# A hybrid decoder trunk on one core: the first modulation summed on two engines and in halves, and the first column block begun on half of the features

## The chip, the cores and the metric

The kernel runs on one core of a Trainium2 chip. A core has TensorE (PE; its weight loads are shown apart as PEld), VectorE (DVE), ScalarE (ACT), GpSimd (POOL), and SyncE (SP), which in this kernel issues every DMA transfer. The metric is the device time of one execution in microseconds (us).

## The reference

One layer over 2048 tokens of 1024 features, batch 1. The part that the change touches is the modulation, the first normalisation and the first projection:

```python
c_act = jax.nn.silu(c)
mod = c_act @ w_ada[l] + b_ada[l]
sh1, sc1, gt1, sh2, sc2, gt2 = [m[:, None, :] for m in jnp.split(mod, 6, axis=-1)]
h = rms_norm(x, g_mix[l]) * (1.0 + sc1) + sh1
p = h @ w_in          # 1024 x 3088, columns shared out among all head groups
```

Behind it come forgetting attention, a chunked mLSTM and a spatial gate over the columns of p, `w_out`, and a ConvFFN with the second modulation. `w_ada` has 1024 rows and 6 x 1024 columns: the first 1024 are the shift `sh1`, the next 1024 the scale `sc1`. All inputs and the output are float32.

## The kernel before

The whole kernel is one stream of instructions for each engine; a scheduler of the framework orders them by priority and dependence, and each engine then runs its own in order. SP keeps eight loads in flight: load number i is issued once load number i - 8 has landed.

**Products.** Each float32 operand of a projection is split into a high part and a rest (`hh` and `hl` for the activations, `whi` and `wlo` for the weights), and `mm3` makes three matmuls of it (lines 54, 55, 56) into one PSUM tile.

**Front.** Four tiles of x (128 tokens x 1024) are loaded and normalised in place (`norm_x`: two squares with a sum on ScalarE, line 498, three small operations, and the product on VectorE, line 503). `first_mod(hf)` (lines 440 to 450) makes shift and scale for features hf * 512 to hf * 512 + 511: for each of the two column ranges, eight tiles `wa` (128 rows of `w_ada` x 512 columns, 256 KB) are loaded; VectorE sums them, weighted by silu(c), into `modacc` (lines 422 and 424); then four matmuls with a column of ones (line 444) sum over the partitions and leave the result as columns. `columns` loads `g_mix` and `b_ada` and transposes them (line 397). VectorE adds the bias (lines 448 to 450) and leaves `sh1` and `a1` (shown as sh and a).

**h tiles.** `make_h(tb, ...)` makes the eight feature tiles k of token block tb (512 tokens): four transposes of x to a PSUM tile (line 542), ScalarE multiplies by `a1` and adds `sh1` (line 546), VectorE makes `hh` (547) and `hl` (548). In token block 0 the PSUM tiles come in turn from `trp` (two buffers) and from `acc` (two buffers and one `acc2`).

**Column blocks.** W_in's columns are taken in 14 blocks, over the first 1024 tokens (half 0) and then over the rest. `w_block` loads a block's weights in two parts `wst` (features 0 to 511 and 512 to 1023); ScalarE makes `whi` (line 569), another engine `wlo` (line 570): GpSimd for the very first block, VectorE for all others. Block 0 of half 0 (272 columns) is `natural` with `use_km`: for each of eight token tiles 8 feature tiles x 3 matmuls of 128 x 272 into one PSUM tile `acc`, an eviction on ScalarE (line 604), a store, and the gates' sum on VectorE (606). Block 1 is `do_qm`. Token block 1's h tiles (x tiles xt4 to xt7) are made between block 0's matmuls. `head_setup` loads a dozen small operands and transposes `wsn`.

**Order of the front before:** `first_mod(0)`, then `w_block(blocks[0][0], G)`, then `first_mod(1)`, then `make_h` of both token blocks with `head_setup` between them, then block 0.

Of the kernel before, what the change touches and what calls it, by code (L numbers as in the profile page):

```python
# [33 lines left out]
def trunk(  # L34
# [403 lines left out]
    modp = mps()  # L438

    def first_mod(hf):  # L440
        for n in (hf, 2 + hf):
            acc = mod_sum(load_ada(n * 512, "hT"))
            for j in range(4):
                T.matmul(modp[:, n * 4 + j : n * 4 + j + 1], acc[:, j * P : (j + 1) * P], ones[:, 0:1], start=True, stop=True)
        if hf == 0:
            columns(colA[:, 0:24], 24, g_mix, b_ada[:, 0:2048])
        sl, o = slice(hf * 4, hf * 4 + 4), hf * 4
        V.tensor_tensor(sh1[:, sl], modp[:, o : o + 4], ba[:, o : o + 4], op=ALU.add)
        V.tensor_tensor(a1[:, sl], modp[:, 8 + o : 12 + o], ba[:, 8 + o : 12 + o], op=ALU.add)
        V.scalar_tensor_tensor(a1[:, sl], a1[:, sl], 1.0, gm[:, o : o + 4], op0=ALU.add, op1=ALU.mult)  # L450
# [86 lines left out]
    def make_h(tb, xin=None):  # L537
        xs = xin if tb == 0 else norm_x(xin or [load_x(tb * 4 + i) for i in range(4)])
        for k in range(KT):
            ps = (tr_ps, acc_ps)[k % 2]() if tb == 0 else tr_ps()  # L540
# [11 lines left out]
    def w_block(parts, eng=V):  # L552

        width = sum(w for _, w in parts)
        tiles = []
        for kp in range(2):
            st = pool.tile([P, 1088], F32, name="wst", tag="wst")
            hi = pool.tile([P, 1088], F32R, name="whi", tag="whi")
            lo = pool.tile([P, 1088], F32R, name="wlo", tag="wlo")
            n = 4 * width  # L560
            v3 = lambda t: t[:, :n].rearrange("p (a b) -> p a b", a=4)
            o = 0
            for col, wd in parts:
                dma(
                    v3(st)[:, :, o : o + wd],
                    w_in[kp * 512 : kp * 512 + 512, col : col + wd].rearrange("(a p) n -> p a n", p=P),
                )
                o += wd
            A.copy(hi[:, :n], st[:, :n])
            eng.tensor_tensor(lo[:, :n], st[:, :n], hi[:, :n].bitcast(F32), op=ALU.subtract)  # L570
            tiles += [(v3(hi)[:, a, :], v3(lo)[:, a, :]) for a in range(4)]
        return tiles, width
# [370 lines left out]
    for n, (half, i) in enumerate(steps):  # L943
        if i == 0:
            make_h(half * 2, x0)
            if half == 0:
                head_setup()
# [658 lines left out]
```

## Time and profile before

| | us |
|---|---|
| median of 3 runs | 2734.72 |
| lowest and highest of the runs | 2733.98, 2736.56 |
| the profiled execution | 2737.65 |
| its span | 2735.9 |

The profiled execution is one of its own, 2.93 us above the median of the runs; 1.75 us of it lie around the span. Its mean granted TensorE clock is 0.978. Busy time is told by engine; times in the timeline count from the start of the span, and a number in brackets there is the time for which the engine stood idle ahead of that row, with what ended it. The front that the change touches is the first 76 us; the rest of the projection, the attention and the ConvFFN follow.

### The profile page before, as it was taken

To read this page: it belongs to the slowest core of one execution; us is meant where nothing else is said; L and a number is where in the kernel's file an instruction comes from. 1 tells how busy PE (TensorE), PEld (TensorE's weight loads), DVE (VectorE), ACT (ScalarE), POOL (GpSimd) and SP (SyncE) were. 2 spreads that over 40 slices of the span, in tenths; PEclk is the share of its full clock that TensorE was granted. 3 is DMA by queue.
4 is the path that set the end of the run, shared out by engine and by line. 5 is a ranking of instruction groups with operands and counts; after the bars stand their busy time and mean duration, and the time that the engine had idled before them with its cause. 6 is when DMAs were issued, how large, how long until landed. Compare 5 with 4: busy or idle time off the path is not lost.

```text
span 2735.9 us, 40287 instructions
## 1 busy us (share of the span) xinstructions
PE 2600.8 (95%) x14345; PEld 2231.9 (82%) x14345; DVE 2009.3 (73%) x3499; ACT 1298.6 (47%) x2448; POOL 459.3 (17%) x592
## 2 busy tenths in 40 slices
PE   5988888989899999999998999999999999999999
PEld 5988888989897788777786888888888888888787
DVE  7356466245446888886668988887988887899797
ACT  4243225233226888884445544444544444444443
POOL 2032221032225566662000000000000000000000
PEclk9988999999999999999999999999999999999999
DMA  7534365424346335625663222228222224849533
GB/s 249 169 102 134 103 183 169 123 53 140 89 139 171 108 108 143 165 56 183 229 242 85 93 90 80 85 82 293 87 78 92 77 85 157 299 137 310 175 108 116
DMA packets 313085, 382.09 MB, mean 140 GB/s; under 512 B 31004, under 2 KB 214264, under 8 KB 310836
## 3 DMA queue, kind: packets, MB, share of 16 engines
q1 hardware_dynamic: 312884, 379.52, 44.2%
q8 instruction: 113, 1.85, 0.3%
q14 instruction: 88, 0.72, 0.1%
HBM read 278.67 MB, written 100.77 MB: 139 GB/s over the span
## 4 chain that ended last, share of the span: by engine, by line
PE 58%; DVE 7%; DMA 2%; ACT 2%; issue 2%; POOL 1%; DVEq 0%; ACTq 0%; SPq 0%; POOLq 0%
PE ub L56 10%; PE ub L55 10%; PE ub L54 10%; PE db L55 4%; PE db L56 4%; PE db L54 4%; PE sp L210 3%; PE tp L263 3%; PE op L249 2%; PE op L250 2%; PE wps L55 2%; PE wps L56 2%; PE wps L54 2%; DVE wspl L1350 2%; DMA wd<-in_w_down_dram 1%
## 5 line engine op out<-in xcount | busy, mean ns | idle before, releaser
L54 PE MATMUL acc<-whi,hh 128*128 128x256 f32 (+1 forms) x1408 | 424.0, 302 | 23.9 <-DVE qn L700 10.8
L56 PE MATMUL acc<-whi,hl 128*128 128x256 f32 (+1 forms) x1408 | 412.0, 294 | 0.5 <-DVE hl L548 0.5
L55 PE MATMUL acc<-wlo,hh 128*128 128x256 f32 (+1 forms) x1408 | 412.2, 293 | 0.0
L54 PEld LDWEIGHTS acc<-whi,hh 128*128 128x128 f32 x1408 | 282.7, 201 | 30.8 <-ACT ev L640 7.5
L55 PEld LDWEIGHTS acc<-wlo,hh 128*128 128x128 f32 x1408 | 283.3, 201 | 0.4 <-issue 0.2
L56 PEld LDWEIGHTS acc<-whi,hl 128*128 128x128 f32 x1408 | 281.9, 201 | 1.3 <-DVE hl L548 0.9
L54 PE MATMUL ub<-T,wsph 128*128 128x512 f32 x704 | 274.2, 390 | 5.8 <-ACT wsph L1218 5.8
L56 PE MATMUL ub<-T,wspl 128*128 128x512 f32 x704 | 273.7, 389 | 0.6 <-DVE wspl L1219 0.6
L55 PE MATMUL ub<-T,wsph 128*128 128x512 f32 x704 | 273.9, 389 | 0.0
L55 PE MATMUL db<-wspl,wsph 128*128 128x512 f32 x616 | 240.4, 390 | 2.7 <-DVE wspl L1350 2.7
L56 PE MATMUL db<-wsph,wspl 128*128 128x512 f32 x616 | 239.6, 389 | 0.0
L54 PE MATMUL db<-wsph 128*128 128x512 f32 x616 | 238.2, 389 | 0.3 <-ACT wsph L1349 0.3
L1218 ACT CAST wsph<-S 128x512 fp32r<-128x512 f32 x176 | 109.7, 623 | 229.6 <-PE ub L55 164.1
L267 DVE TENSOR_TENSOR plo<-tp,phi 128x512 fp32r<-128x512 f32 (+1 forms) x320 | 186.8, 607 | 34.6 <-ACT phi L266 32.6
L54 PE MATMUL ub<-B,wsph 128*128 128x512 f32 x528 | 207.1, 392 | 2.8 <-ACT wsph L1218 2.8
L56 PE MATMUL ub<-B,wspl 128*128 128x512 f32 x528 | 207.0, 392 | 0.7 <-DVE wspl L1219 0.7
L55 PE MATMUL ub<-B,wsph 128*128 128x512 f32 x528 | 206.8, 392 | 0.0
L227 ACT ACTIVATE L<-L,nm 128x1024 f32<-128x1024 f32 (+2 forms) x192 | 172.5, 902 | 33.5 <-DVE nm L216 32.1
L263 PE MATMUL tp<-ident,L 128*128 128x128 f32 x1088 | 180.4, 278 | 3.8 <-POOL L L232 1.2
L266 ACT CAST phi<-tp 128x512 fp32r<-128x512 f32 (+1 forms) x320 | 160.4, 521 | 45.2 <-PE tp L263 43.8
L210 PE MATMUL sp<-kk,q 128*128 128x512 f32 (+3 forms) x640 | 169.3, 376 | 2.4 <-DVE nm L216 1.5
L232 POOL TENSOR_SCALAR L<-L,rs 128x1024 f32<-128x1024 f32 (+2 forms) x192 | 167.2, 881 | 11.2
(334 smaller groups left out, 5891.1 us busy)
## 6 DMA issues: line engine op xcount, KB each, us to landing
w<-in_w_up_dram SPq DMA_DIRECT2D x88, 512.0 KB
wd<-in_w_down_dram SPq DMA_DIRECT2D x176, 256.0 KB
wa<-in_w_ada_dram SPq DMA_DIRECT2D x96, 256.0 KB
wst<-in_w_in_dram SPq DMA_DIRECT2D x48, 512.0 KB
act_d<-yc SPq DMA_DIRECT2D x44, 512.0 KB
act<-act_d SPq DMA_DIRECT2D x44, 512.0 KB
q<-q_d SPq DMA_DIRECT2D x128, 128.0 KB
hc_d<-hl SPq DMA_DIRECT2D x28, 512.0 KB
```

Of the source, the lines that this page charges most:

```text
L54: T.matmul(ps, lh, rh, start=start, stop=False, skip_group_check=resume)
L55: T.matmul(ps, lh, rl, start=False, stop=False, skip_group_check=resume)
L56: T.matmul(ps, ll, rh, start=False, stop=stop, skip_group_check=resume)
L210: T.matmul(sp[:, b : b + bw], q2[n][:, qs], kk[:, s0 + b : s0 + b + bw], start=n == 0, stop=n == 1 and not last)
L227: A.activation(L[c], L[c], AF.Exp, bias=nm[:, n - 1 : n], scale=-1.0, accum_out=rs[:, c : c + 1])
L232: G.tensor_scalar(t, t, rs[:, 0:1], 1.0, op0=ALU.mult, op1=ALU.mult)
L249: T.matmul(op[:, c0:], vv[:, j, :], hi[:, c0:], start=(j == 0), stop=False)
L250: T.matmul(op[:, c0:], vv[:, j, :], lo[:, c0:], start=False, stop=(j == ns - 1))
L263: T.transpose(tp[:, i * P : (i + 1) * P], rows[i][j // 8][:, (j % 8) * P : (j % 8 + 1) * P], ident)
L266: A.copy(hi[:, c0:], tp[:, c0:])
L267: V.tensor_tensor(lo[:, c0:], tp[:, c0:], hi[:, c0:].bitcast(F32), op=ALU.subtract)
L1218: A.copy(hi, src)
```

## The change

`first_mod` loads the shift's and the scale's tiles in turn and keeps the sixteen of a half together. VectorE sums the shift's as before. The scale is summed on TensorE: a 128 x 128 piece of `wa` is the stationary operand, the column of silu(c) that belongs to its rows the moving one, and the eight row tiles accumulate in PSUM (line 451 of the changed kernel), two columns of the result at a time, in a tile `mps` and a tile `mp`; VectorE adds the bias to each (line 454). `columns` of `g_mix` and `b_ada` goes ahead of the tiles. `make_h` takes a range of feature tiles. Token block 0's feature tiles 0 to 3 are made after the first half; the first part of block 0's weights follows, and the matmuls of feature tiles 0 to 3 of three token tiles (36, into all three `acc` buffers); then `first_mod(1)`, the second part of the weights, and feature tiles 4 to 7. `natural` goes on with the three begun PSUM tiles. `wlo` of the first block is made on VectorE. Line numbers of the changed kernel are higher by 10 in `make_h` (542 is 552, 546 is 556), by 8 in the split of the weights (569 is 577, 570 is 578) and by 17 in `use_km` (604 is 621).

```diff
@@ -435,19 +435,29 @@
         V.tensor_scalar(gq8, colA[:, 32:33], 0.125, None, op0=ALU.mult)
 
 
-    modp = mps()
 
     def first_mod(hf):
-        for n in (hf, 2 + hf):
-            acc = mod_sum(load_ada(n * 512, "hT"))
-            for j in range(4):
-                T.matmul(modp[:, n * 4 + j : n * 4 + j + 1], acc[:, j * P : (j + 1) * P], ones[:, 0:1], start=True, stop=True)
         if hf == 0:
             columns(colA[:, 0:24], 24, g_mix, b_ada[:, 0:2048])
-        sl, o = slice(hf * 4, hf * 4 + 4), hf * 4
-        V.tensor_tensor(sh1[:, sl], modp[:, o : o + 4], ba[:, o : o + 4], op=ALU.add)
-        V.tensor_tensor(a1[:, sl], modp[:, 8 + o : 12 + o], ba[:, 8 + o : 12 + o], op=ALU.add)
-        V.scalar_tensor_tensor(a1[:, sl], a1[:, sl], 1.0, gm[:, o : o + 4], op0=ALU.add, op1=ALU.mult)
+        o = hf * 4
+
+        ws = [(next(a_), next(b_)) for a_, b_ in [(load_ada(hf * 512, "hT"), load_ada((2 + hf) * 512, "hT"))] for _ in range(KT)]
+        acc = mod_sum(w for w, _ in ws)
+        for pair in range(2):
+            ps = [mps(), misc_ps()]
+            for k in range(KT):
+                for i in range(2):
+                    c = (2 * pair + i) * P
+                    T.matmul(ps[i][:, 0:1], ws[k][1][:, c : c + P], cs[:, k : k + 1], start=k == 0, stop=k == KT - 1)
+            for i in range(2):
+                c = o + 2 * pair + i
+                V.tensor_tensor(a1[:, c : c + 1], ps[i][:, 0:1], ba[:, 8 + c : 9 + c], op=ALU.add)
+        ps = mps()
+        for j in range(4):
+            T.matmul(ps[:, j : j + 1], acc[:, j * P : (j + 1) * P], ones[:, 0:1], start=True, stop=True)
+        V.tensor_tensor(sh1[:, o : o + 4], ps[:, 0:4], ba[:, o : o + 4], op=ALU.add)
+        sl = slice(o, o + 4)
+        V.scalar_tensor_tensor(a1[:, sl], a1[:, sl], 1.0, gm[:, sl], op0=ALU.add, op1=ALU.mult)
 
     def rest_of_mod(n):
 
@@ -534,10 +544,10 @@
 
     hT = {}
 
-    def make_h(tb, xin=None):
+    def make_h(tb, xin=None, ks=range(KT)):
         xs = xin if tb == 0 else norm_x(xin or [load_x(tb * 4 + i) for i in range(4)])
-        for k in range(KT):
-            ps = (tr_ps, acc_ps)[k % 2]() if tb == 0 else tr_ps()
+        for k in ks:
+            ps = (tr_ps, acc_ps)[k % 2]() if tb == 0 and ks[0] == 0 else tr_ps()
             for i in range(4):
                 T.transpose(ps[:, i * P : (i + 1) * P], xs[i][:, k * P : (k + 1) * P], ident)
             h32 = pool.tile([P, TB], F32, name="h32", tag="t2k")
@@ -549,27 +559,27 @@
             hT[tb, k] = (hh, hl)
 
 
-    def w_block(parts, eng=V):
+    def w_part(parts, kp, eng=V):
 
         width = sum(w for _, w in parts)
-        tiles = []
-        for kp in range(2):
-            st = pool.tile([P, 1088], F32, name="wst", tag="wst")
-            hi = pool.tile([P, 1088], F32R, name="whi", tag="whi")
-            lo = pool.tile([P, 1088], F32R, name="wlo", tag="wlo")
-            n = 4 * width
-            v3 = lambda t: t[:, :n].rearrange("p (a b) -> p a b", a=4)
-            o = 0
-            for col, wd in parts:
-                dma(
-                    v3(st)[:, :, o : o + wd],
-                    w_in[kp * 512 : kp * 512 + 512, col : col + wd].rearrange("(a p) n -> p a n", p=P),
-                )
-                o += wd
-            A.copy(hi[:, :n], st[:, :n])
-            eng.tensor_tensor(lo[:, :n], st[:, :n], hi[:, :n].bitcast(F32), op=ALU.subtract)
-            tiles += [(v3(hi)[:, a, :], v3(lo)[:, a, :]) for a in range(4)]
-        return tiles, width
+        st = pool.tile([P, 1088], F32, name="wst", tag="wst")
+        hi = pool.tile([P, 1088], F32R, name="whi", tag="whi")
+        lo = pool.tile([P, 1088], F32R, name="wlo", tag="wlo")
+        n = 4 * width
+        v3 = lambda t: t[:, :n].rearrange("p (a b) -> p a b", a=4)
+        o = 0
+        for col, wd in parts:
+            dma(
+                v3(st)[:, :, o : o + wd],
+                w_in[kp * 512 : kp * 512 + 512, col : col + wd].rearrange("(a p) n -> p a n", p=P),
+            )
+            o += wd
+        A.copy(hi[:, :n], st[:, :n])
+        eng.tensor_tensor(lo[:, :n], st[:, :n], hi[:, :n].bitcast(F32), op=ALU.subtract)
+        return [(v3(hi)[:, a, :], v3(lo)[:, a, :]) for a in range(4)]
+
+    def w_block(parts):
+        return w_part(parts, 0) + w_part(parts, 1), sum(w for _, w in parts)
 
     pending = []
     background = []
@@ -580,15 +590,22 @@
         if background and (pool.has("att_r") or ticks[0] * 4 % 7 < 4) and next(background[0], True):
             background.pop(0)
 
-    def natural(half, wb, consume):
+    def nat_mm(ps, tt, tiles, width, ks=range(KT)):
+        tb, o = tt // 4, (tt % 4) * P
+        for k in ks:
+            hh, hl = hT[tb, k]
+            mm3(ps[:, :width], hh[:, o : o + P], hl[:, o : o + P], tiles[k][0], tiles[k][1], k == 0, k == KT - 1)
+
+    def natural(half, wb, consume, begun=()):
         tiles, width = wb
         for i in range(8):
             tt = half * 8 + i
-            tb, o = tt // 4, (tt % 4) * P
-            ps = acc_ps()
-            for k in range(KT):
-                hh, hl = hT[tb, k]
-                mm3(ps[:, :width], hh[:, o : o + P], hl[:, o : o + P], tiles[k][0], tiles[k][1], k == 0, k == KT - 1)
+            if i < len(begun):
+                ps = begun[i]
+                nat_mm(ps, tt, tiles, width, range(4, KT))
+            else:
+                ps = acc_ps()
+                nat_mm(ps, tt, tiles, width)
             tick()
             late = consume(tt, ps)
             if late is not None:
@@ -938,13 +955,21 @@
     nb = len(blocks)
     steps = [(h, i) for h in range(2) for i in range(nb)]
     rest = [2, 3, 4, 5, 0, 1, 6, 7]
-    wb = w_block(blocks[0][0], G)
+
+    make_h(0, x0, range(4))
+    wb = w_part(blocks[0][0], 0), 272
+    begun = [acc_ps() for _ in range(3)]
+    for tt in range(3):
+        nat_mm(begun[tt], tt, *wb, range(4))
     first_mod(1)
+    wb = wb[0] + w_part(blocks[0][0], 1), 272
     for n, (half, i) in enumerate(steps):
         if i == 0:
-            make_h(half * 2, x0)
             if half == 0:
+                make_h(0, x0, range(4, KT))
                 head_setup()
+            else:
+                make_h(half * 2, x0)
             make_h(half * 2 + 1)
         elif n == nb - 1:
             x0 = [load_x(8 + t) for t in range(4)]
@@ -965,7 +990,10 @@
         cur = wb
         if n + 1 < len(steps):
             wb = w_block(blocks[steps[n + 1][1]][0])
-        blocks[i][1](half, cur)
+        if n == 0:
+            natural(0, cur, use_km, begun)
+        else:
+            blocks[i][1](half, cur)
         if i == 1:
             log_gates(half)
         if i == 3:
```

Three places, from the instruction lists of the two kernels (a row's number counts the rows of its engine; x8 means eight alike in a row; names are output<-inputs).

TensorE, from the transposes of x2 (k = 0 to 3) to the end of the first half's sums. Before:

```order
14 L542 MATMUL trp<-ident,xt 128x128
15 L542 MATMUL acc<-ident,xt 128x128
16 L542 MATMUL trp<-ident,xt 128x128
17 L542 MATMUL acc<-ident,xt 128x128 x2
18 L444 MATMUL mps<-ones,modacc 128x1 x8
19 L397 MATMUL mp<-ident,rows 128x24
20 L444 MATMUL mps<-ones,modacc 128x1 x4
21 L542 MATMUL trp<-ident,xt 128x128 x4
```

And in the changed kernel (cs is silu(c)):

```order
14 L552 MATMUL acc<-ident,xt 128x128
15 L451 MATMUL mps<-cs,wa 128x1
16 L451 MATMUL mp<-cs,wa 128x1
17 L451 MATMUL mps<-cs,wa 128x1
18 L552 MATMUL trp<-ident,xt 128x128
19 L552 MATMUL acc<-ident,xt 128x128
20 L552 MATMUL trp<-ident,xt 128x128
21 L552 MATMUL acc<-ident,xt 128x128
22 L451 MATMUL mps<-cs,wa 128x1
23 L451 MATMUL mp<-cs,wa 128x1
24 L451 MATMUL mps<-cs,wa 128x1 x2
25 L451 MATMUL mp<-cs,wa 128x1
```

Twenty-one of the first half's 24 matmuls of the first three columns stand behind the four transposes of x3; the rest of them follows in the same pattern.

TensorE, from the end of the first half to the begun matmuls, in the changed kernel:

```order
36 L451 MATMUL mps<-cs,wa 128x1
37 L457 MATMUL mps<-ones,modacc 128x1 x4
38 L451 MATMUL mp<-cs,wa 128x1 x8
39 L552 MATMUL trp<-ident,xt 128x128 x8
40 L54 MATMUL acc<-whi,hh 128x272 x3
41 L55 MATMUL acc<-wlo,hh 128x272
42 L56 MATMUL acc<-whi,hl 128x272
```

Behind the 36 begun matmuls (rows 40 to 73) the second half's sums stand in the same order: 24 of line 451, four of line 457, eight of line 451, and then the transposes of k = 6. The four transposes of k = 4 and of k = 5 are row 39.

ScalarE, from the first h tile. Before:

```order
6 L569 CAST whi<-wst 128x1088 x2
7 L546 ACTIVATE h_384<-trp,sh_90,a_89 128x512
8 L546 ACTIVATE h_395<-acc,sh_90,a_89 128x512
9 L546 ACTIVATE h_406<-trp,sh_90,a_89 128x512
10 L546 ACTIVATE h_417<-acc,sh_90,a_89 128x512
11 L546 ACTIVATE h_428<-trp,sh_90,a_89 128x512
```

And in the changed kernel:

```order
6 L556 ACTIVATE h_335<-trp,sh_90,a_89 128x512
7 L556 ACTIVATE h_346<-acc,sh_90,a_89 128x512
8 L556 ACTIVATE h_357<-trp,sh_90,a_89 128x512
9 L556 ACTIVATE h_368<-acc,sh_90,a_89 128x512
10 L577 CAST whi<-wst 128x1088 x2
11 L556 ACTIVATE h_520<-trp,sh_90,a_89 128x512
```

The two casts of block 0's weights stand behind four h tiles where they stood ahead of them. VectorE's two splits stand there behind the fourth `hh`, and its second half's sums behind the splits.

Further on, the evictions of token tiles 0 and 1 stand on ScalarE ahead of the squares of xt5, where before one eviction stood there; on TensorE nine matmuls of one token tile lie between the last six groups of four transposes of xt4 to xt7, where before the matmuls of two token tiles were interleaved with them. On SP eight small loads of `head_setup` (g_ffn to gmo) stand ahead of the second half's sixteen `wa`, where they stood behind them, and `columns` of `g_mix` and `b_ada` ahead of the first half's.

## The prediction

> **What bounds the kernel now.** I read the page first, then the stretches of the front, then its timeline.
>
> ```profile
> span 2735.9 us, 40287 instructions
> PE 2600.8 (95%) x14345; PEld 2231.9 (82%) x14345; DVE 2009.3 (73%) x3499; ACT 1298.6 (47%) x2448; POOL 459.3 (17%) x592
> ```
>
> TensorE is busy for 95% of the span, so there is time to win where it stands idle. The next view cuts the front into stretches: length, then busy time (and instructions) of PE, PEld, DVE, ACT and POOL, granted clock, DMA share, GB/s.
>
> ```profile
> 0.00:20.00 20.00, 6.65 (x27) 4.99 (x27) 13.09 (x39) 7.86 (x19) 5.20 (x14) 1.00 0.91 332
> 20.00:35.00 15.00, 2.87 (x13) 2.64 (x13) 12.31 (x19) 3.64 (x4) 5.61 (x2) 1.00 0.99 333
> 35.00:40.00 5.00, 4.53 (x20) 4.13 (x20) 4.89 (x9) 1.25 (x2) 0.00 (x0) 1.00 0.19 53
> 43.00:50.00 7.00, 6.96 (x29) 6.01 (x29) 6.29 (x16) 2.78 (x4) 2.31 (x4) 0.51 0.99 364
> 60.00:76.35 16.35, 16.33 (x130) 15.90 (x129) 10.72 (x23) 8.73 (x14) 0.00 (x0) 1.00 0.44 132
> ```
>
> From 20 to 35 us TensorE works 2.87 of 15 us while the DMA engines are 99% busy: the front is a load. From 43 to 50 it is busy at a granted clock of 0.51; from 60 on it is full (16.33 of 16.35). My yardstick is the first matmul of `do_qm`, since behind it the order of instructions stays nearly as it was and TensorE is the bound:
>
> ```profile
> 76.35 0.40 PE L54 MATMUL acc<-hh,whi 128*128 128x512 f32 x1
> ```
>
> The timeline of the front (start, length, engine, line; in brackets the idle time before and who ended it):
>
> ```profile
> 14.80 0.75 DVE L503 TENSOR_SCALAR xt<-xt,st 128x1024 f32<-128x1024 f32 x1 [0.44 <-POOL st L132]
> 15.61 0.47 PE L542 MATMUL trp<-ident,xt 128*128 128x128 f32 x1 [1.39 <-DVE xt L503]
> 18.10 8.23 DVE L424 SCALAR_TENSOR_TENSOR modacc<-wa,cs,modacc 128x512 f32<-128x512 f32 x8
> 19.24 10.85 SPq L414 DMA_DIRECT2D wa<-in_w_ada_dram  x16
> 23.05 5.61 POOL L570 TENSOR_TENSOR wlo<-wst,whi 128x1088 fp32r<-128x1088 f32 x2 [8.29 <-ACT whi L569]
> 23.48 2.85 DVE L424 SCALAR_TENSOR_TENSOR modacc<-wa,cs,modacc 128x512 f32<-128x512 f32 x1
> 23.80 1.10 ACT L569 CAST whi<-wst 128x1088 fp32r<-128x1088 f32 x1 [0.82 <-DMA wst<-in_w_in_dram]
> 29.26 0.78 ACT L546 ACTIVATE h<-trp,sh,a 128x512 f32<-128x512 f32 x1 [4.37 <-DVE a L450]
> 29.60 5.47 DVE L424 SCALAR_TENSOR_TENSOR modacc<-wa,cs,modacc 128x512 f32<-128x512 f32 x7
> 41.61 0.74 DVE L424 SCALAR_TENSOR_TENSOR modacc<-wa,cs,modacc 128x512 f32<-128x512 f32 x1
> 44.72 0.78 ACT L546 ACTIVATE h<-trp,sh,a 128x512 f32<-128x512 f32 x1 [4.42 <-DVE a L450]
> ```
>
> The first h waits until 29.26 for VectorE's sums, although SP, which keeps eight loads in flight, was issuing the second half's at 19.24. At 10.85/16 = 0.68 us a load the first half's last tile landed at about 19.9; VectorE ended 6.4 us later (18.10 + 8.23 = 26.33). The fifth feature tile waits until 44.72 for sums that end at 42.35.
>
> **The change part by part.**
>
> *What is taken away.* Eight sums of a half leave VectorE, 5.47/7 = 0.78 us each, and one stall: the sum at 23.48 took 2.85, in the time of GpSimd's splits of the weights (23.05 to 28.66), which now go to VectorE. [...]
>
> *What a one-column matmul costs.* In their place TensorE gets 32 matmuls a half, of the form of line 444: 128 x 128 stationary, one column moving, float32.
>
> ```profile
> L444 PE MATMUL mps<-ones,modacc 128*128 128x1 f32 x32 | 6.8, 333 | 14.5 <-DVE modacc L424 14.5
> 26.39 1.87 PE L444 MATMUL mps<-ones,modacc 128*128 128x1 f32 x8 [5.62 <-DVE modacc L424]
> 42.41 1.17 PE L444 MATMUL mps<-ones,modacc 128*128 128x1 f32 x8 [0.27 <-DVE modacc L424]
> 168.84 1.11 PE L471 MATMUL mp<-ones,modacc 128*128 128x1 f32 x8
> ```
>
> The code issues 16 of them (four for each of four column ranges), and the profile records 32: two records each. So four cost 1.87 us at the low clock and 1.17 or 1.11 at the full one: 0.47 and 0.29 us each. 32 of them and the shift's 4 are 16.8 us of TensorE for a half at the low clock and 10.4 at the full one, against 12 to 14 us of VectorE's sums that they spare in both halves together (16 x 0.78 and the stall). That is the term that decides.
>
> *First half.* TensorE takes its work in order: by after's list only three scale matmuls come before the last four transposes of k = 0 to 3, which wait for x3 (normalised at 15.55, transposed from 15.61). So 21 remain at 16.4. A pair of loads lands every 1.36 us, three matmuls cost 1.41 at the low clock, and TensorE now ends after the loads: 21 x 0.47 = 9.9 to 26.3 all low. If it comes to the full clock after 7 us, as in the stretches at 43 and at 207 (below), 14 are done by 23 and 7 x 0.29 more make 25.0. Then four of the shift (1.17) and eight of the second pair (2.34): 28.5, 0.6 for the bias: first h at 29.1. Bounds: 27.6 with the full clock from 19 on; 32.5 all low. So VectorE's 26.33 becomes TensorE's 28.5, and the first h is where it was.
>
> *Begun matmuls.* ScalarE's four h (4 x 0.78) end at 32.2, and the cast of the weights, which stood at 23.80 or before, now stands behind them: 33.3. VectorE's split goes from there to 34.7:
>
> ```profile
> 59.26 1.22 DVE L570 TENSOR_TENSOR wlo<-wst,whi 128x1024 fp32r<-128x1024 f32 x1
> 48.36 0.43 PE L54 MATMUL acc<-whi,hh 128*128 128x272 f32 x1
> 48.59 0.43 PE L55 MATMUL acc<-wlo,hh 128*128 128x272 f32 x1
> 52.95 0.29 PE L54 MATMUL acc<-whi,hh 128*128 128x272 f32 x1
> 53.08 0.29 PE L55 MATMUL acc<-wlo,hh 128*128 128x272 f32 x1
> ```
>
> Starts 0.23 us apart at the low clock, 0.13 at the full one. 33 of the 36 need that split. TensorE has been thin from 29 to 34.7, and rows behind an idle stretch show the low clock for 7 us, so they end at 42.1 (39.0 and 42.3 as ends).
>
> ```profile
> 203.00:207.00 4.00, 0.06 (x1) 0.09 (x1) 2.73 (x10) 1.08 (x2) 1.60 (x2) 1.00 0.32 108
> 207.00:214.00 7.00, 7.00 (x36) 6.88 (x37) 5.58 (x12) 0.00 (x0) 2.87 (x2) 0.51 0.59 174
> ```
>
> *Second half.* Its loads, eight small ones ahead of them, have landed by about 37 (24.2 + 16 x 0.68 + 1.8) and VectorE's sums by 43, so nothing but TensorE holds it: 24 x 0.29 = 7.0 to 49.1, 1.17, 2.34, 0.6: h4 at 53.2, where before it came at 44.72. All low it is 42.3 + 36 x 0.47 + 0.6 = 59.8, and 62.9 with the late first half; all full, from a first h at 27.6, 48.7. What keeps the clock in these 10 us is not shown: the only rows of this form are eight records long. I take 54.5, nearer the full end, since the matmuls before them are dense.
>
> *From h4 to block 1.* ScalarE and VectorE carry it to the transposes of the last x tile (the first two rows are one feature tile's hh and hl):
>
> ```profile
> 47.81 0.42 DVE L547 CAST hh<-h 128x512 fp32r<-128x512 f32 x1
> 48.26 0.69 DVE L548 TENSOR_TENSOR hl<-h,hh 128x512 fp32r<-128x512 f32 x1
> 52.23 0.36 ACT L604 COPY ev<-acc 128x256 f32<-128x256 f32 x1
> 52.36 0.16 DVE L499 TENSOR_TENSOR st<-st 128x1 f32<-128x1 f32 x1 [2.34 <-ACT jk L498]
> 53.37 0.75 DVE L503 TENSOR_SCALAR xt<-xt,st 128x1024 f32<-128x1024 f32 x1 [0.47 <-POOL st L132]
> 58.59 0.75 DVE L503 TENSOR_SCALAR xt<-xt,st 128x1024 f32<-128x1024 f32 x1 [0.65 <-POOL st L132]
> 59.40 0.44 PE L542 MATMUL trp<-ident,xt 128*128 128x128 f32 x2
> ```
>
> Before: 59.40 - 44.72 = 14.7, with (58.59 - 53.37)/3 = 1.74 a tile. Now two evictions stand on ScalarE ahead of xt5's squares and wait for token tiles 0 and 1: 37 matmuls and transposes at 0.13 or 0.23 and 0.5 for the last h, 5.3 or 9.0 us. Then 2 x 0.36, squares 1.7, norm 1.0, 2 x 1.74, 0.8: 13.0 or 16.7, and 14.0 taken. From there to do_qm it was 76.35 - 59.40 = 17.0; now 96 matmuls and 24 transposes, 120 x 0.126 (16.35/130) = 15.1 of work, but only nine matmuls lie between the six last groups of transposes, which VectorE paces at about 1.1 us (hh 0.42, hl 0.69): 6 x 1.1 + 87 x 0.126 = 17.6, ends 15.1 and 21 (7 us at half clock). The 36 matmuls that are done early save nothing, since this chain hides them.
>
> *Sum.* 54.5 + 14.0 + 17.6 = 86.1 against 76.35: 9.7 us more. The ends are 48.7 + 13.0 + 16.3 = 78.0 and 62.9 + 16.7 + 17.6 = 97.2, 1.7 and 20.9 more. The profiled execution took 2737.65 us for a span of 2735.9, 2.9 above the median of 2734.72; I put the difference on the median: **2744.4 us**, 0.35% slower. A measurement of this kernel tells about 0.2%, 5.5 us.
>
> **The rivals.**
>
> *The low clock holds.* If one-column matmuls do not count as work for the clock, the first h comes at 32.5, the begun matmuls end near 45, the sums run low: h4 at 62, 62 + 14.9 + 17.6 = 94.5: 18 us more, 2752.9. For it: at 18.90 and 26.39 line 444 runs low. Against it: those follow idle time.
>
> *The full clock holds.* TensorE is dense from 15.6 on; at the full clock from 19 it makes h4 at 49 and do_qm at 49 + 13.0 + 16.3 = 78.3: 2736.7, no change that can be told. [...] The rows at 43 and 207 show 7 us at 0.51.
>
> *The one-column matmul costs one record.* If two records overlap when sums alternate between two PSUM tiles, each costs 0.23 or 0.146: the first half follows the loads (first h 24.1, 5.2 us earlier), the begun matmuls end at 36.5, h4 comes at 42.0, do_qm at 42.0 + 14.8 + 17.6 = 74.4: 2.0 us less, 2732.7, faster. It decides below about 0.25 us each. Against it: 1.87 for eight records, back to back, is already with the weight loads beside them.
>
> **How the numbers follow.** My forecast (2739 to 2749) 0.52, low clock 0.20, full clock 0.18, one record 0.10. Slower by over 0.2% (above 2740.2): 0.47 of mine, the low clock's 0.20 and 0.07 of the full clock's if the chain behind h4 is slow too. Faster by over 0.2%: 0.04 of the one-record case, where its clock is full. The rest, 0.22, is within. Range 2735.5 to 2754: it leaves out the one-record case and the last of the low clock. My forecast's own range is 2739 to 2749.
>
> **What would show it.** Line 451 near 0.6 to 0.9 us for two instructions; the first h at 28 to 32 and not 24; TensorE busy with the sums behind the landed loads; no first-half sum of VectorE above 1 us; h4 later than 48; two evictions ahead of xt5's squares; do_qm near 86 and the end shifted by the same. I am wrong if h4 comes before 46, or if the end shifts otherwise than do_qm does.

## The result and the profile after

The changed kernel takes 2742.99 us (median of 8 runs, 2739.59 to 2745.44); the kernel before, run beside it, 2735.69 (2733.98 to 2739.68). The ratio is 1.0024, with a 95% interval of 1.0013 to 1.0035: 7.3 us slower, and the interval stays above 1. The ratios further down leave out one execution, e9's of 4249.45 us at a mean granted clock of 0.558. The profiled execution took 2742.07 us, with a span of 2740.3 and a mean granted clock of 0.975.

| point in the trace, us | before | after | predicted |
|---|---|---|---|
| first h tile (k = 0) | 29.26 | 29.64 | 29.1 |
| begun matmuls end | none | 40.89 | 42.1 |
| h4, the fifth h tile | 44.72 | 52.92 | 54.5 |
| first matmul of `do_qm` | 76.35 | 84.52 | 86.1 |
| last matmul into `acc`, the projection's end | 830.7 | 836.5 | |

The page of after: its span and busy times.

```profile
span 2740.3 us, 40504 instructions
PE 2620.9 (96%) x14457; PEld 2253.8 (82%) x14457; DVE 2004.3 (73%) x3491; ACT 1298.8 (47%) x2448; POOL 453.0 (17%) x590
```

TensorE gains 20.1 us of busy time and the span 4.4; VectorE loses only 5.0. Where the 20 us stand, the stretches of after's front tell (columns as in the prediction):

```profile
15.00:29.00 14.00, 14.00 (x68) 14.00 (x66) 4.87 (x10) 0.00 (x0) 0.00 (x0) 1.00 0.85 257
40.90:45.00 4.10, 4.10 (x40) 4.10 (x38) 2.01 (x3) 0.00 (x0) 2.07 (x4) 1.00 0.57 204
45.00:52.50 7.50, 7.41 (x36) 7.32 (x35) 0.69 (x5) 0.00 (x0) 0.00 (x0) 0.51 0.00 0
```

From 15 to 29 us, where TensorE used to stand idle most of the time, it is busy for 14.00 of 14 us, and from 40.9 to 52.4 again. In the last 7.5 us of that no transfer runs and VectorE works 0.69: TensorE alone holds the fifth feature tile. The timeline of the same stretch:

```profile
13.28 0.75 DVE L513 TENSOR_SCALAR xt<-xt,st 128x1024 f32<-128x1024 f32 x1 [0.66 <-POOL st L132]
15.08 0.42 PE L451 MATMUL mps<-cs,wa 128*128 128x1 f32 x2
25.61 3.55 PE L451 MATMUL mp<-cs,wa 128*128 128x1 f32 x16
29.19 0.16 DVE L454 TENSOR_TENSOR a<-mp,colA 128x1 f32<-128x1 f32 x1 [3.25 <-PE mp L451]
29.64 0.78 ACT L556 ACTIVATE h<-trp,sh,a 128x512 f32<-128x512 f32 x1 [18.13 <-DVE a L460]
35.32 0.60 PE L55 MATMUL acc<-wlo,hh 128*128 128x272 f32 x1 [0.81 <-DVE wlo L578]
37.51 5.48 DVE L424 SCALAR_TENSOR_TENSOR modacc<-wa,cs,modacc 128x512 f32<-128x512 f32 x7
37.98 0.42 PE L55 MATMUL acc<-wlo,hh 128*128 128x272 f32 x1
38.37 0.29 PE L54 MATMUL acc<-whi,hh 128*128 128x272 f32 x1
40.89 0.28 PE L451 MATMUL mps<-cs,wa 128*128 128x1 f32 x2
45.05 0.54 PE L451 MATMUL mp<-cs,wa 128*128 128x1 f32 x2
48.86 3.55 PE L451 MATMUL mp<-cs,wa 128*128 128x1 f32 x16
52.92 1.45 ACT L556 ACTIVATE h<-trp,sh,a 128x512 f32<-128x512 f32 x2 [18.50 <-DVE a L460]
67.94 0.44 PE L552 MATMUL trp<-ident,xt 128*128 128x128 f32 x2 [0.74 <-DVE xt L513]
84.52 0.40 PE L54 MATMUL acc<-hh,whi 128*128 128x512 f32 x1
```

Both h tiles wait for an add that waits for line 451 (at 29.19 the bracket says so: 3.25 us, PE). Between 15.08 and 29.16 (25.61 + 3.55) stand 33 one-column matmuls, 66 records: 0.213 us a record, 0.43 a matmul. From 40.89 to 45.05 it is 38 records in 4.16 us, 0.109 each; then 34 in 7.36, 0.216. So the sums ran at the low clock through the first half, at the full one for 4.2 us behind the dense matmuls, and low again. The trace's own list of clock changes agrees: its first entry is a rise to the full clock at 38.27 us, and at 45.10 it falls to half. (The granted clock of the first stretch above reads 1.00 all the same; the last section says why.) VectorE's sums of the second half had ended at 42.99 (37.51 + 5.48).

### The profile page after: what moved, and what is told of

It reads as the page before. It is cut to its first block, busy times and chain, and to the rows that moved or that the text cites. A ratio compares the mean times of both kernels' runs of the same rounds, so it can differ in the third digit from the quotient of the medians.

```text
span 2740.3 us, 40504 instructions
## 1 busy us (share of the span) xinstructions
PE 2620.9 (96%) x14457; PEld 2253.8 (82%) x14457; DVE 2004.3 (73%) x3491; ACT 1298.8 (47%) x2448; POOL 453.0 (17%) x590
## 3 DMA queue, kind: packets, MB, share of 16 engines
q8 instruction: 114, 1.87, 0.3%
## 4 chain that ended last, share of the span: by engine, by line
PE 57%; DVE 6%; DMA 2%; ACT 2%; issue 2%; POOL 1%; SPq 0%; DVEq 0%; ACTq 0%; POOLq 0%
PE ub L56 10%; PE ub L54 10%; PE ub L55 10%; PE db L55 4%; PE db L56 4%; PE db L54 4%; PE sp L210 3%; PE tp L263 3%; PE op L249 2%; PE op L250 2%; DVE wspl L1378 1%; PE wps L55 1%; PE wps L54 1%; PE wps L56 1%; ACT L L227 1%
## 5 line engine op out<-in xcount | busy, mean ns | idle before, releaser
L232 POOL TENSOR_SCALAR L<-L,rs 128x1024 f32<-128x1024 f32 (+2 forms) x192 | 167.3, 882 | 11.2
```

The costliest lines, as they stand in the source:

```text
L232: G.tensor_scalar(t, t, rs[:, 0:1], 1.0, op0=ALU.mult, op1=ALU.mult)
```

## The experiments

The question is what makes h4, and with it `do_qm`, 8.2 us later. Theory A of the expectations is TensorE's time for the one-column matmuls; theory B is the halves themselves, with what they put ahead of the second half's sums; theory D, which came in with the later runs, is that the second half's loads come late. All runs in one table, times in us, each ratio against runs of the kernel before on the same chip:

| run | first h | h4 | `do_qm` | projection's end | ratio (95%) |
|---|---|---|---|---|---|
| before | 29.26 | 44.72 | 76.35 | 830.7 | |
| after | 29.64 | 52.92 | 84.52 | 836.5 | 1.0024 (1.0013 to 1.0035) |
| e1_scale_on_vector | 26.98 | 51.48 | 82.69 | 834.3 | 1.0024 (1.0015 to 1.0033) |
| e2_sum_alone | 29.91 | 49.13 | 83.16 | 835.9 | 1.0032 (1.0021 to 1.0042) |
| e3_wide | 24.26 | 48.32 | 81.69 | 835.2 | 1.0013 (1.0004 to 1.0022) |
| e4_row | 25.17 | 49.73 | 80.06 | 837.2 | 1.0028 (1.0017 to 1.0039) |
| e6_loads_ahead | 29.58 | 58.71 | 89.96 | 839.2 | 1.0046 (1.0032 to 1.0061) |
| e7_vector_loads_ahead | 26.98 | 49.60 | 82.60 | 833.3 | 1.0022 (1.0011 to 1.0032) |
| v1_row_loads_ahead | 25.97 | 46.29 | 77.47 | 831.4 | 0.9999 (0.9988 to 1.0011) |
| v2_rows_loads_ahead | 31.77 | 52.65 | 84.21 | 841.4 | 1.0032 (1.0020 to 1.0045) |
| v3_row_setup_later | 25.27 | 45.68 | 75.68 | 833.9 | 1.0008 (0.9998 to 1.0018) |
| b1_setup_later | 29.39 | 45.47 | 76.95 | 830.5 | 1.0004 (0.9994 to 1.0013) |
| e8_half_the_sums | 25.93 | 45.69 | 77.14 | 832.0 | 1.0004 (0.9994 to 1.0014) |
| e9_eight_columns | 29.56 | 55.80 | 87.30 | 841.8 | 1.0034 (1.0019 to 1.0050) |

### e1_scale_on_vector: the halves, with the scale back on VectorE

```diff
         acc = mod_sum(w for w, _ in ws)
-        for pair in range(2):
...
+        acc2 = mod_sum(w for _, w in ws)
         ps = mps()
+        for n, a in enumerate((acc, acc2)):
+            for j in range(4):
+                T.matmul(ps[:, 4 * n + j : 4 * n + j + 1], a[:, j * P : (j + 1) * P], ones[:, 0:1], start=True, stop=True)
...
```

> The changed kernel with the scale summed on VectorE again, as the shift is (16 sums a half, 8 ones-matmuls a half); the halves, the begun matmuls and the order of loads stay. Theory A (the loss is the time that TensorE spends on one-column matmuls ahead of the h tiles): the first h comes near 28 as VectorE ends its 16 sums near 26, the second half waits for VectorE (16 sums of 0.78 from about 35, then 8 ones-matmuls): h4 near 49.5 against 52.9 after the change, do_qm near 81, about 3.5 us less than the change and still 4 to 5 us more than before. Theory B (the loss lies in the halves and the begun matmuls, wherever the scale is summed): do_qm at 84 to 85 as after the change. Theory C (TensorE's sums are the whole loss): do_qm at or before 76.4.

`do_qm` stays 6.3 us late without any of the scale matmuls: 82.69 lies between the 81 of theory A and the 84 to 85 of theory B, and far from the 76.4 of theory C. The timeline of this run:

```profile
34.33 0.88 DVE L422 TENSOR_SCALAR modacc<-wa,cs 128x512 f32<-128x512 f32 x2
38.97 0.17 DVE L400 COPY colA<-mp 128x14 f32<-128x14 f32 x1 [3.10 <-PE mp L397]
39.78 8.16 DVE L424 SCALAR_TENSOR_TENSOR modacc<-wa,cs,modacc 128x512 f32<-128x512 f32 x12
47.33 3.57 PE L450 MATMUL mps<-ones,modacc 128*128 128x1 f32 x16 [8.40 <-DVE modacc L424]
51.48 1.45 ACT L550 ACTIVATE h<-trp,sh,a 128x512 f32<-128x512 f32 x2 [19.74 <-DVE a L454]
```

VectorE comes to the second half's sums at 34.33, behind the first half's `hh`, `hl` and the weights' split, and then stands 3.10 us at a copy of other columns (line 400), for a transpose that TensorE has behind the begun matmuls. Twelve sums follow until 47.94, then 16 records at the low clock. So the halves have a price of their own on VectorE, as long as it has all sixteen sums of a half to make.

### e2_sum_alone: the sums on TensorE, without the halves

`first_mod` is the changed one; everything behind it is the kernel before:

```diff
-    make_h(0, x0, range(4))
-    wb = w_part(blocks[0][0], 0), 272
...
+    wb = w_block(blocks[0][0], G)
     first_mod(1)
-    wb = wb[0] + w_part(blocks[0][0], 1), 272
...
```

> The kernel before with the new first_mod alone: TensorE sums the scale, loads in turn; no halves of the h tiles, no begun matmuls, the first weights' split on GpSimd. Theory A: 72 instructions of two records at 0.21 to 0.23 each stand in TensorE's order ahead of the fifth h tile; the first half ends near 29 as after the change, the second near 48 to 50, do_qm at 80 to 83, 4 to 7 us more than before. Theory B: do_qm near 76.4, as before. Either way VectorE has no sum of 2.85 us unless GpSimd still splits beside the sums.

That part alone costs 6.8 us at `do_qm`, 4.4 of them at h4. The timeline of this run shows the one-column matmuls ending the wait again: the last column's 16 records, then the shift's eight, all at the low clock.

```profile
43.63 3.41 PE L450 MATMUL mp<-cs,wa 128*128 128x1 f32 x16
46.90 1.84 PE L456 MATMUL mps<-ones,modacc 128*128 128x1 f32 x8
49.13 0.78 ACT L555 ACTIVATE h<-trp,sh,a 128x512 f32<-128x512 f32 x1 [12.51 <-DVE a L459]
```

The other 2.4 us arise behind h4; ScalarE stands 5.30 us there, up to 57.22, at a copy for which TensorE transposes `wsn`, but how much of the 2.4 us that makes was not tried.

Each part alone loses 6.3 to 6.8 us and both together 8.2, not 13: h4 waits for whichever of TensorE and VectorE ends last, so the two prices do not add up.

### e8_half_the_sums: half of the one-column matmuls

The scale is summed over every second row tile only, so over half of the rows; loads and all the rest stay.

```diff
-            for k in range(KT):
+            for k in range(1, KT, 2):
...
```

> The changed kernel with the scale summed over every second row tile only (16 instead of 32 one-column matmuls a half); loads, order and everything else stay, so the scale it uses is another. Theory A (the one-column matmuls' time on TensorE is the loss): 16 x 0.44 less before the first h, bounded by the loads: first h near 25 instead of 29.6; h4 near 44 instead of 52.9, since the loads and VectorE's sums now hold it; do_qm near 76, about 8 us less than the changed kernel and as before. Theory B (the halves and the begun matmuls are the loss): do_qm at 82 or later.

The timeline of this run:

```profile
23.60 1.84 PE L451 MATMUL mp<-cs,wa 128*128 128x1 f32 x8
25.93 0.78 ACT L556 ACTIVATE h<-trp,sh,a 128x512 f32<-128x512 f32 x1 [14.44 <-DVE a L460]
43.34 1.84 PE L451 MATMUL mp<-cs,wa 128*128 128x1 f32 x8
45.69 1.45 ACT L556 ACTIVATE h<-trp,sh,a 128x512 f32<-128x512 f32 x2 [14.99 <-DVE a L460]
77.14 0.40 PE L54 MATMUL acc<-hh,whi 128*128 128x512 f32 x1
```

With 32 of the 64 matmuls gone, h4 comes 7.2 us earlier and `do_qm` 7.4, and the loss can no longer be told (1.0004). Nothing else in the program was edited. This shows theory A for the changed kernel: TensorE's time for the one-column matmuls is what the change loses. What is left of the halves' price, with eight sums a half on VectorE, is small: h4 is 1.0 us and `do_qm` 0.8 us behind the kernel before. Even here TensorE ends last, at 45.18 (43.34 + 1.84), where the expectation had the loads and VectorE's sums.

### e3_wide: the same matmuls with 128 columns

The silu column is broadcast to 128 columns, of which one is used: the same number of matmuls, but more work in each.

```diff
+    NW = 128
...
-                    T.matmul(ps[i][:, 0:1], ws[k][1][:, c : c + P], cs[:, k : k + 1], start=k == 0, stop=k == KT - 1)
+                    T.matmul(ps[i][:, 0:NW], ws[k][1][:, c : c + P], cs[:, k : k + 1].broadcast_to([P, NW]), start=k == 0, stop=k == KT - 1)
```

> The changed kernel with the moving operand of the scale's matmuls made 128 columns wide, the same column 128 times (of which one is used); the same number of matmuls and stationary loads. After the change TensorE stood at the low clock from 13 to 29 us though it was busy for 8.00 of 8 us. Theory A1 (one column moving does not count as work for the clock, streamed columns do): these matmuls come to the full clock within 7 us, spacing of a record 0.14 from about 22 on instead of 0.21, the first half ends 2 to 3 us earlier, do_qm near 78 to 80. Theory A2 (the clock goes by how busy the engine is, whatever it streams, or the low clock there has another cause): records stay at 0.21 to 0.23 and do_qm at 84 to 86.

It does more and is sooner done. The timeline of this run, from its first half to its fifth h tile:

```profile
16.07 1.02 PE L453 MATMUL mps<-cs,wa 128*128 128x128 f32 x4
17.16 0.61 PE L453 MATMUL mps<-cs,wa 128*128 128x128 f32 x4
21.75 2.03 PE L453 MATMUL mp<-cs,wa 128*128 128x128 f32 x16
24.26 0.78 ACT L558 ACTIVATE h<-trp,sh,a 128x512 f32<-128x512 f32 x1 [0.99 <-DVE a L462]
27.21 12.04 SPq L414 DMA_DIRECT2D wa<-in_w_ada_dram  x16
44.37 0.49 PE L453 MATMUL mps<-cs,wa 128*128 128x128 f32 x2 [0.48 <-DMA wa<-in_w_ada_dram]
48.32 1.45 ACT L558 ACTIVATE h<-trp,sh,a 128x512 f32<-128x512 f32 x2 [1.42 <-PE mp L397]
```

Sixteen records take 2.03 us where one-column ones took 3.55, and the four that took 1.02 at 16.07 take 0.61 a microsecond later: the engine has come to the full clock. At the low clock a record costs the same with 128 columns as with one (four took 0.99 in after, at 15.79). First h is 5.4 us earlier. The second half gains less, 4.6, since the order of SP moved too: its loads begin at 27.21, where after has them from 24.08, and the last sums wait for them (at 44.37). So `do_qm` missed the 78 to 80 of theory A1, though the clock did what A1 says. The time lies between before and after, but its interval overlaps with that of after.

### e9_eight_columns: the same with eight columns

As in e3_wide, with `NW = 8`; this keeps the order of the changed kernel on each engine.

> The changed kernel with eight equal moving columns instead of one in the scale's matmuls; every engine's order is that of the changed kernel. In the run with 128 columns the clock came up about 4 us after these matmuls began; that run also moved xt4's load and the casts. Theory A1 (the clock follows how much of the time columns stream; 8 columns are under 5% of a record of 0.22 us): the clock stays low as after the change, first h near 29.6, h4 near 53, do_qm at 84 to 85. Theory A3 (any width over one does): records fall to 0.14 from about 19 on, first h near 26, do_qm below 81.

Eight columns did not lift the clock here: the 16 records of 25.51, of eight columns, take 3.56 us, where 16 of one column took 3.55 in after. The stretches of this run:

```profile
15.00:29.00 14.00, 14.00 (x67) 13.97 (x66) 4.78 (x10) 0.00 (x0) 0.00 (x0) 1.00 0.80 247
44.50:55.20 10.70, 10.70 (x51) 10.70 (x51) 0.64 (x4) 0.00 (x0) 0.00 (x0) 0.50 0.00 0
```

The 14 us of the first half look as in after, and from 44.5 on TensorE is busy all the time at 0.50. Here the begun matmuls ended 1.1 us later than in after (42.0), since the clock rose only at 40.87 and not at 38.27; the low clock came back sooner behind them (from 44.2), and h4 is 2.9 us later still.

### e6_loads_ahead and e7_vector_loads_ahead: the second half's loads first

In e6 the sixteen loads of the second half go ahead of the first half's sums (`first_load` holds the line that fills `ws`); e7 does the same to e1.

```diff
-    first_mod(0)
+    columns(colA[:, 0:24], 24, g_mix, b_ada[:, 0:2048])
+    ld0 = first_load(0)
...
-    make_h(0, x0, range(4))
     wb = w_part(blocks[0][0], 0), 272
+    ld1 = first_load(1)
+    first_mod(0, ld0)
+    make_h(0, x0, range(4))
...
-    first_mod(1)
+    first_mod(1, ld1)
```

> The changed kernel with the second half's sixteen loads issued ahead of the small loads of head_setup and of the second part of the weights, and the first part's cast ahead; the one-column sums stay on TensorE. After the change these loads began at 24.1 behind the small ones. Theory A (TensorE's one-column sums at the low clock hold the second half, not its loads): h4 at 50 to 54, do_qm at 82 to 85, time within 2 us of the changed kernel. Theory D (the late loads hold it): h4 before 47, do_qm before 79.

> The same with the scale summed on VectorE: loads of the second half ahead, no one-column sums on TensorE but the eight of line 444's kind a half. Theory A, extended by the run with VectorE's sums (a half's sums stand in an engine's order behind the other half's h tiles): VectorE has 16 sums of 0.76, eight casts and differences and two splits of the weights from 27 on, 19 us, then the ones-matmuls at the low clock, 3.6: h4 near 49 to 51, do_qm at 80 to 83. Theory D: h4 near 44, do_qm near 76.

Theory D falls for the changed kernel and for e1: e6 is the slowest of all, and e7 is where e1 is. (Theory A's 50 to 54 for h4 in e6 is missed too.) The timeline of e6 tells why:

```profile
39.49 0.56 PE L451 MATMUL mps<-cs,wa 128*128 128x1 f32 x2
43.46 0.42 PE L451 MATMUL mps<-cs,wa 128*128 128x1 f32 x2
47.24 0.16 DVE L454 TENSOR_TENSOR a<-mps,colA 128x1 f32<-128x1 f32 x1 [7.64 <-PE mps L451]
55.74 0.75 DVE L424 SCALAR_TENSOR_TENSOR modacc<-wa,cs,modacc 128x512 f32<-128x512 f32 x1
58.71 1.44 ACT L557 ACTIVATE h<-trp,sh,a 128x512 f32<-128x512 f32 x2 [21.12 <-DVE sh L458]
```

With the tiles there earlier, the scheduler mixes the second half's sums with the begun matmuls. The add of line 454 then waits 7.64 us for TensorE, and behind it on VectorE stand the last sums of the shift, until 56.49. VectorE works in order here, so the wait of one add is lent to all that stands behind it.

### e4_row: the scale as a row

The silu column is the stationary operand and 512 columns of `wa` move: eight matmuls a half in place of 32, then ScalarE copies the row and four small matmuls turn it.

```diff
...
+        pr = misc_ps()
+        for k in range(KT):
+            T.matmul(pr[0:1, :], cs[:, k : k + 1], ws[k][1], start=k == 0, stop=k == KT - 1)
+        row = pool.tile([1, 512], F32, name="row", tag="t2k")
+        A.copy(row, pr[0:1, :])
         ps = mps()
+        for j in range(4):
+            T.matmul(ps[:, 4 + j : 5 + j], row[:, j * P : (j + 1) * P], ones[0:1, 0:1], start=True, stop=True)
...
```

> The changed kernel with the operands of the scale's matmuls exchanged: silu(c)'s column is stationary and a whole 128 x 512 tile of the weights moves, 8 matmuls a half instead of 32, into one row; a copy on ScalarE and 4 matmuls with one row turn the row into columns. Theory A: TensorE's sums follow the loads; 8 matmuls of two records at 0.43 a record at the low clock are 7 us a half against 14, the first h comes near 25 to 26, h4 near 43, do_qm near 73 to 76: at least 8 us less than the change, and 0 to 3 us less than before. Theory B: do_qm near 84.

The timeline of this run: its records stand 0.43 us apart, 0.86 a row tile, where four one-column matmuls took 4 x 0.43 = 1.7 in the first half of after.

```profile
15.81 6.17 PE L448 MATMUL mp<-wa,cs 128*1 128x512 f32 x14
45.52 1.02 PE L448 MATMUL mp<-wa,cs 128*1 128x512 f32 x2 [0.34 <-DMA wa<-in_w_ada_dram]
```

That is not half the work, but another clock, and the expectation, which took 0.43 a record for the low clock, was wrong in this. By the trace's list the clock of e4 was full from 15.48 to 25.72; at the full clock four one-column matmuls take 8 x 0.109 = 0.87 us, as much as the row. At the low clock the row takes 1.7 too, as the timeline of v2 (below) shows, whose clock rises at 15.83: a row tile takes 1.71 at 12.66 and 0.85 at 16.82, from start to start.

```profile
12.66 1.91 PE L448 MATMUL mp<-wa,cs 128*1 128x512 f32 x2
14.37 1.75 PE L448 MATMUL mps<-wa,cs 128*1 128x512 f32 x2
16.82 1.02 PE L448 MATMUL mps<-wa,cs 128*1 128x512 f32 x2
17.67 1.02 PE L448 MATMUL mp<-wa,cs 128*1 128x512 f32 x2
```

So in the first half e4 gains by the clock, as e3 does. First h comes at 25.17, but the last tile of the second half is waited for at 45.52, its loads having begun at 27.04 behind small ones: in e3 and e4, unlike in after, the late loads do hold h4. `do_qm` is 3.7 us late, where 73 to 76 were expected, and the time 0.28% longer, 7.7 us: the widest gap between the two in all runs.

### v1, v2, v3 and b1: looking for a version that gains

v1 is e4 with the loads of e6. v2 sums the shift as a row on TensorE too:

```diff
-        acc = mod_sum(w for w, _ in ws)
-        pr = misc_ps()
+        prs = [mps(), misc_ps()]
         for k in range(KT):
-            T.matmul(pr[0:1, :], cs[:, k : k + 1], ws[k][1], start=k == 0, stop=k == KT - 1)
+            for n in range(2):
+                T.matmul(prs[n][0:1, :], cs[:, k : k + 1], ws[k][n], start=k == 0, stop=k == KT - 1)
...
```

v3 is v1 with most of `head_setup` moved behind block 0, and b1 is that move alone, in the kernel before:

```diff
     def head_setup():
-        rest_of_columns()
-        dma(gsgu, g_sgu.broadcast_to([P, 256]))
-        dma(gmo, g_m_out.broadcast_to([P, 256]))
...
+
+    def head_late():
+        rest_of_columns()
+        dma(gsgu, g_sgu.broadcast_to([P, 256]))
+        dma(gmo, g_m_out.broadcast_to([P, 256]))
```

> The row form (8 matmuls of 512 columns a half) with the second half's loads ahead. In the run of the row form the first h came at 25.2, but the second half's last load landed only near 45 because xt4 and fourteen small loads stood ahead of it. Theory A and the loads together: last load near 33, h4 near 38 to 40, do_qm at 68 to 72, 5 to 8 us less than before the change, time 2727 to 2731. If the halves and the begun matmuls cost something by themselves (theory B): do_qm at or above 76.

> As the run before, with the shift too as a row on TensorE: 16 matmuls of 512 columns a half and no sum on VectorE. They take 14 us a half at the low clock (0.43 a record) and 7 at the full one, against 10.9 us of loads; TensorE streams columns, so the clock should be full in the second half: first h near 26, h4 near 37 to 40, do_qm at 67 to 72, time 2726 to 2731. If TensorE's time per half is again the bound: h4 above 43.

> The row form with the second half's loads ahead, and of head_setup only gbias in the front; its other loads, transposes and copies come after column block 0. In the run before this one VectorE stood from 38 to 41.7 behind a copy of head_setup's columns with four sums still to do, and h4 came at 46.3. If that was the hold: VectorE ends its sums near 39 to 40, h4 at 41 to 43, do_qm at 70 to 74, 2 to 6 us less than before the change. Rival: the halves lose again what the sums win, since the chain over ScalarE from h4 to the last x tile takes its 14 to 15 us: do_qm no earlier than 75.

> The kernel before with the same part of head_setup moved behind column block 0, and nothing else: it tells how much of the run beside it comes from that alone. TensorE was full from 50.2 on before, so little is expected: h4 at 44 to 45, do_qm at 74 to 76.5, time within 2 us of before. If the small loads and their transposes held the front: do_qm below 73.

None of v1, v2 and v3 came to the 67 to 74 that were hoped for at `do_qm`. v1 ends level with the kernel before (0.9999). The timeline of v1 has the next wait:

```profile
40.55 1.05 PE L453 MATMUL mps<-ones,row 1*128 1x1 f32 x8
41.71 0.17 DVE L400 COPY colA<-mp 128x14 f32<-128x14 f32 x1 [3.69 <-PE mp L397]
42.58 1.54 DVE L424 SCALAR_TENSOR_TENSOR modacc<-wa,cs,modacc 128x512 f32<-128x512 f32 x2
```

The scale is ready at 41.6, but VectorE has stood 3.69 us at line 400, with three sums of the shift behind it (41.80, and two at 42.58). v3 takes that copy away, and another wait is there, in the timeline of v3:

```profile
35.10 1.10 ACT L579 CAST whi<-wst 128x1088 fp32r<-128x1088 f32 x1 [7.05 <-DMA wst<-in_w_in_dram]
36.23 1.29 DVE L580 TENSOR_TENSOR wlo<-wst,whi 128x1088 fp32r<-128x1088 f32 x1 [3.50 <-ACT whi L579]
42.09 0.75 DVE L424 SCALAR_TENSOR_TENSOR modacc<-wa,cs,modacc 128x512 f32<-128x512 f32 x1
```

VectorE waits 3.50 us for the split of weights that landed late. h4 is still 1.0 us behind the kernel before, `do_qm` 0.7 ahead of it, and the time is not (1.0008). b1 moves nothing. v2 loses as after does: with 16 matmuls of 512 columns a half, at 0.86 us each though the clock is full from 15.83 on, TensorE is the hold again, and first h comes at 31.77. No version tried beats the kernel before.

## Why the prediction was right

It was right in direction and in reason, and near in size: 9.7 us more were predicted and 7.3 measured; TensorE's one-column matmuls carry the loss, as e8 shows. That the 2744.4 us predicted and the 2742.99 measured lie so close is in part luck, since the steps err in both directions. Point by point:

- **Yardstick.** `do_qm` is 8.2 us later and the time 7.3 longer; predicted were 9.7 for both. Over the runs the two go together, from v1 to e6, but not to better than about 5 us: between `do_qm` and the end of the projection the shift against before changes by -5.1 us (e6) to +3.9 (v3).
- **What leaves VectorE.** The stall is gone: the seven sums at 37.51 take 0.78 us each, and no sum of the first half is above that. Why the sum at 23.48 took 2.85 us beside GpSimd's splits was not shown.
- **The price of a one-column matmul was too high.** The step divided the length of a group's row by its records (1.87 us for eight). Such a row ends with the whole length of its last record (in after, the eight records at 23.90 last 1.84 us, and the next row starts 1.71 behind them). From start to start a matmul costs 0.43 us at the low clock, not 0.47, and 0.22 at the full one, not 0.29. The two records of each matmul are as predicted, which ends the rival of one record.
- **First half.** "If it comes to the full clock after 7 us" is a step that failed: the clock stayed low for all 14 us. First h still came at 29.64, near the 29.1 of the forecast, by luck: two errors worked against this one, the smaller price and an earlier start: x3 is normalised at 13.28, since VectorE has fewer sums ahead of it, so the 33 matmuls begin at 15.08, where 16.4 was said.
- **Begun matmuls.** They reach the full clock 2.9 us after 35.32 (rows 0.22 us apart until 38.2, 0.12 from 38.37), not after 7, and end at 40.89 instead of 42.1.
- **Second half.** "All full" makes 53.2 by the forecast's prices and "all low" 59.8; 54.5 was taken between. It ran full for 4.2 us and low for 7.4, at smaller prices, and h4 came at 52.92. By the measured prices all full would be 40.89 + 72 x 0.109 + 0.5 = 49.2 and all low 40.89 + 72 x 0.213 + 0.5 = 56.7, so in the second half alone the low clock costs 3.7 us. The loads (24.1 + 11.2 + 1.8 = 37.1) and VectorE's sums (42.99) were out of the way, as said.
- **From h4 on.** 31.6 us were predicted and 31.60 measured, but as 15.0 and 16.6 where 14.0 and 17.6 stood. Before it was 31.63: the 36 matmuls done early save nothing here, as the forecast said. The ends of the forecast's sum took 16.3 and 17.6 for the last term, though its own ends were 15.1 and 21; with those they would be 76.8 and 100.6.
- **The rivals.** The low clock's case did happen in both parts: one-column matmuls did not bring the full clock in the 14 us of the first half (0.213 us a record), and behind the begun ones it lasted 4.2 us. Its price of 18 us did not, since the begun matmuls brought the clock up and the matmul was cheaper; a first h at 32.5 and h4 at 62 are refuted. The full clock's case is not seen in after; e3 is the nearest to it, with records 0.11 us apart from 16.9 on and with h4 at 48.32 (49 was said). The full clock from 19 on, which that case and the bound of 27.6 for the first h (and so the sum's end of 78.0) assume, is the author's estimate, and no run with the scale's one-column matmuls shows it: in after the clock rose at 38.27.

What was not foreseen is that the halves lose by themselves (e1): the prediction counted them as the same work in another order. That price belongs to sixteen sums a half on VectorE; with the eight of the changed kernel little of it is left (e8). Open are the 4 us of e4, and what raises the clock. From `do_qm` to the projection's end the clock is low for 88.7 us before and for 95.6 in e4, which takes 2.8 us longer for that part; but it is low for 95.6 in e7 too, which takes 3.7 us less, so the low stretches alone do not explain it.

## What to carry to other kernels

A product of a matrix with one vector is not cheap for having one moving column: here a record took about 0.21 us at the low clock with one column, with eight and with 128. The 33 matmuls of the first half took 14 us, more than the 6.2 us (8 x 0.78) of the VectorE sums that they replaced. With the vector as the stationary operand TensorE needed as long at the same clock (0.86 us a row tile at the full one, against 0.87), but it came to the full one in the first half (at 15.48 in e4). Before a sum is moved to an idle engine, price the whole of it at the clock which that engine will have, from start to start of the rows, and look at what stands behind each new wait in the order of both engines. When the parts of a change each lose the same few microseconds at one join, their prices do not add (6.3 and 6.8 us here, and 8.2 together), and undoing one part shows only the other.

## What the runs showed of the hardware

**Busy was not enough for the full clock.** In after TensorE was busy for 14.00 of 14 us with one-column float32 matmuls and stayed at 0.213 us a record; with eight columns (e9) it was busy for 14.00 of 14 too, at the same 0.213; with 128 columns (e3) the records came down from 0.21 to 0.11 about 3.8 us after the first of them at 13.1. In the traces of before and after every stretch between two clock changes is a whole multiple of 3.41 us (3.41 and 6.83 are the first two of before, 6.83 and 13.65 those of after; the last one is cut off by the end). The clock's rise did not come a fixed time behind the first dense matmul: from the first of the dense begun rows shown (35.32 in after) it took 2.9 us, and from the same row 3.8 in e1, 5.6 in e9 and 6.0 in e8.

**Nor did such matmuls keep it.** Back to back behind dense ones, one-column matmuls ran at the full clock for another 4.2 us in after (40.89 to 45.05) and eight-column ones for 2.2 us in e9 (42.0 to 44.2), then fell to a granted 0.51 and 0.50. The full clock had lasted 6.83 us in after (38.27 to 45.10) and 3.42 in e9 (40.87 to 44.29).

**The granted clock's column can miss it.** In after it shows 1.00 from 15 to 29 us, where the records stand 0.213 us apart, and 0.51 from 45 to 52.5, where they stand 0.216 apart. The first entry in the trace's list of clock changes is the rise at 38.27 us (39.79 in the kernel before), and the column shows 1.00 for what lies ahead of it; so the 1.00 that the prediction's first view shows up to 35 us says nothing of the clock. The distance of the records tells it: with one column 0.213 us at the low clock, 0.109 at the full one.
